# Products with zeros on TensorE in the waits of a decoder step's first projection

## The chip, the cores and the metric

One Trainium2 chip, all 8 of its cores, each with its own share of the tokens and the same program. The metric is device microseconds (us) of the slowest core of an execution. The kernel before takes 744.38 us (median of 3 executions, 744.08 to 744.72).

A program on all cores has a second, slower state in some executions, in which the cores of one die (0 to 3 or 4 to 7) run at a lower granted clock. Only fast executions are compared below, except where a table says that it reads the cores of the undisturbed die.

The engines: PE is TensorE (matmuls and transposes), DVE is VectorE, ACT is ScalarE, POOL is GpSimd, SP issues DMA. "Granted clock" is the profile's figure for PE's clock, as a share of the full one. I call a stretch of PE cold when its 128x512 matmuls start 0.43 us apart (core 2 of before: eleven in 4.90 us at 26.47 us) and warm when they start 0.216 us apart (eight in 1.89 us at 87.02 us).

## The reference

One layer of a hybrid decoder. Only the beginning matters here:

```python
mod = (jax.nn.silu(c) @ w_ada + b_ada)[:, None, :]            # shift, scale, gate, twice
sh1, sc1, gt1, sh2, sc2, gt2 = jnp.split(mod, 6, axis=-1)
h = rmsnorm(x, g_pre_mix) * (1 + sc1) + sh1
proj = h @ w_in                                                # the first projection
v_pool, x_conv, gate_b, gate_c = jnp.split(proj, ...)          # pooling mixer | gated short conv
y_pool = pool_mixer(...); y_conv = gate_b * causal_dwconv(gate_c * x_conv, conv_w)
x = x + gt1 * rmsnorm(concat(y_pool, y_conv) @ w_out, g_post_mix)
# ... then a gated FFN with its own short conv: ~600 us of the ~742, untouched by the change
```

The tokens of a core come in 17 tiles of 128 rows and fewer. A tile is loaded (`big<-x`), its squares are summed on ACT, it is scaled on DVE (`xn`), turned by eight transposes on PE, and copied out of PSUM into `ah`. Matmuls of `ah` with the weights (`ring`) follow. Between them stand small "scale products" of the conditioning vector (`sc`) with weights `wsc_0` to `wsc_7`, each of which is needed before its part of the projection can start.

## The kernel before

The kernel is written as a list of operations with their data; a list scheduler of its own puts them in order with a model of their costs, and each engine's list is then emitted strictly in that order, with semaphore waits.

```python
    def emit(self, eng, e):                     # one engine's instructions, in the scheduler's order
        waited = {}
        for o in self.ops[eng]:
            need = {}
            for d in o.deps: ...                # highest count needed of each semaphore
            for s, v in need.items():
                if waited.get(s, 0) < v:
                    e.wait_ge(s.h, v)
                    waited[s] = v
            r = o.fn(e)
```

```python
    # order(): before 70 us of model time a load also waits for the load that landed last in the model
                if o.dma:
                    under += o.nbytes
                    if last is not None and t <= self.UNTIL:
                        o.deps.add(last)
```

```python
    def load_x(t, src_d, reads=(), deps=()):    # a tile of x into one of six buffers in turn
        i = turn(xts)
        load(BIG[i][0:rows, :], src_d[r0:r0 + rows, :], [r_big[i]], rows * 4096, ...)
        return i

    def stats(src, rows, k, t, reads, junk, junk_regs):      # ACT: sum of squares, then the root
        act(junk, src, AF.Square, reads, [r_stat[k][t]] + junk_regs, D, accum=STAT[0:rows, k, t:t + 1])
        act(STAT[0:rows, k + 1, t:t + 1], STAT[0:rows, k, t:t + 1], AF.Sqrt, ...)

    def turn_tile(t, j, eng):                                # PE: eight transposes into one PSUM bank
        b = take()
        psb = PSF[:, b, :].bitcast(BF16).rearrange("p (k n) -> p k n", k=KC)
        tr([psb[:, kc, 0:rows] for kc in range(KC)], [XN[j][...] for kc in range(KC)], IDB, ..., [r_bank[b]], 0.5)
        ...                                                  # copy to AH on ACT or DVE
        give(b)

    def conv_mid(j, c, bs):                                  # first step of the gated conv: ACT empties a bank
        bx, bc, bb = bs
        act(XC[k], PSF[:, bx, :], AF.Identity, [r_bank[bx], r_cb[j]], [r_xc[k]], n, bias=hx)
        give(bx)                                             # the next product may have this bank
        ...
```

All eight banks of the kernel's PSUM tensor (`PSF`, 128 x 8 x 512) are in use through the `take()` and `give()` of such steps. `give(bx)` is why a transpose on PE can have to wait for a copy on ACT (1.31 us on core 2 and 5.30 us on core 7, below).

Of the kernel before, what the change touches and what calls it, by code (L numbers as in the profile page):

```python
# [10 lines left out]
BF16 = mybir.dt.bfloat16  # L11
# [5 lines left out]
KC = 8  # L17
# [41 lines left out]
class Region:  # L59


    __slots__ = ("w", "r", "bank")
# [14 lines left out]
class Sem:  # L77
    __slots__ = ("h", "count")
# [4 lines left out]


class Op:
    __slots__ = ("eng", "fn", "deps", "sig", "need", "dma", "sem", "n", "cost", "nbytes", "idx", "key", "start", "end", "port")


class Sched:
# [8 lines left out]
    def _mk(self, eng, fn, reads, writes, deps, cost):  # L98
        o = Op()
        o.eng, o.fn, o.cost = eng, fn, cost  # L100
        o.sig, o.need, o.dma, o.sem, o.n, o.nbytes = None, False, False, None, 0, 0
        o.port = eng == "pool"
        o.idx = len(self.all)
        d = set(deps)
        for r in reads:
            if r.w is not None:
                d.add(r.w)
            if r.bank:
                d.update(x for x in r.r if x.eng != eng)
        for w in writes:  # L110
            if w.w is not None:
                d.add(w.w)
            d.update(w.r)
        for r in reads:
            r.r.append(o)
        for w in writes:
            w.w = o
            w.r = []
        d.discard(o)
        o.deps = d  # L120
        self.all.append(o)
        return o
# [12 lines left out]

    RATE = 300e3
    DMA_IN, DMA_OUT = 2.0, 1.5
    LIMIT, SHARE, SMALL, UNTIL = 3.0e6, 0.6e6, 0.4e6, 70.0

    def order(self):  # L140
# [99 lines left out]
                done(o)  # L240
        self.makespan = t

    def finalize(self, esems):
        self.order()
        for o in self.all:
            if o.eng == "pe":
                o.deps = {d for d in o.deps if d.eng != "pe"}
        for o in self.all:
            for d in o.deps:
                d.need = True  # L250
        for e in self.ENGS:
            cnt = 0
            for o in self.ops[e]:
                if o.need and not o.dma:
                    cnt += 1
                    o.sig = (esems[e], cnt)

    def emit(self, eng, e):
        waited = {}
        for o in self.ops[eng]:  # L260
            need = {}
            for d in o.deps:
                s, v = d.sig
                if need.get(s, 0) < v:
                    need[s] = v
            for s, v in need.items():
                if waited.get(s, 0) < v:
                    e.wait_ge(s.h, v)
                    waited[s] = v
            if o.fn is None:  # L270
                continue
            r = o.fn(e)
            if o.dma:
                assert len(r) == o.n, (len(r), o.n)
                for i in r:
                    i.then_inc(o.sem.h, 16)
            elif o.need:
                r.then_inc(o.sig[0].h, 1)


def build_program():
# [42 lines left out]
    def alloc(name, shape, dtype, at=None):  # L324
        esz = 4 if dtype == F32 else 2
        n = esz
        for s in shape[1:]:
            n *= s
        n = (n + 31) // 32 * 32
        off = cur[0] if at is None else at  # L330
        if at is None:
            cur[0] += n
        assert off + n <= SB_HI, ("SBUF overflow", name, off + n - SB_HI)
        high[0] = max(high[0], off + n)
        k = names.get(name, 0)
        names[name] = k + 1
        return slab("%s_%d" % (name, k), list(shape), dtype, offset=off)[:]
# [3 lines left out]
    SC = alloc("sc", [128, KC, 18], BF16)  # L341
# [34 lines left out]
    XN = [alloc("xn", [128, D], BF16) for _ in range(NXN)]  # L376
# [13 lines left out]
    VS = alloc("vs", [128, 4, NS, PB + DS], F32)  # L390
    POOLW = alloc("poolw", [128, 4, 128], BF16)
    CTS = alloc("cts", [128, KC * 18], F32, at=gt_at)
    p1_end = cur[0]

    cur[0] = mark
# [15 lines left out]
    PSF = es.enter_context(nc.psum_tensor("ps", [128, 8, 512], F32))  # L411

    def new_sem(name):
        return Sem(es.enter_context(nc.semaphore(name)))
# [7 lines left out]
    esems = {e: new_sem("e_" + e) for e in Sched.ENGS}  # L422
    K = Sched()
# [12 lines left out]
    def c_mm(n, k=1):  # L436
        return k * max(0.03, n / 2400.0 + 0.0025)

    bank_free = list(range(8))
    r_bank = [R(bank=True) for _ in range(8)]  # L440
# [3 lines left out]
    def take():  # L444
        for b in bank_free:
            if b in singles:
                bank_free.remove(b)
                return b
        raise AssertionError("out of PSUM banks")
# [9 lines left out]
    def give(*bs):  # L459
        for b in bs:  # L460
            assert b not in bank_free
            bank_free.append(b)

    def mm(bank_ap, pairs, reads, writes, n, first=True, last=True):
        def fn(e):
            inst = None
            for i, (l, r) in enumerate(pairs):
                inst = e.matmul(bank_ap, l, r, start=(first and i == 0), stop=(last and i == len(pairs) - 1))  # L468
            return inst
        return K.op("pe", fn, reads=reads, writes=writes, cost=c_mm(n, len(pairs)))  # L470

    def tr(outs, ins, ident, reads, writes, cost):
        def fn(e):
            inst = None
            for o, i in zip(outs, ins):
                inst = e.transpose(o, i, ident)  # L476
            return inst
        return K.op("pe", fn, reads=reads, writes=writes, cost=cost)
# [28 lines left out]
    def load(dst, src, regs, nbytes, eng="sp", sem=None, reads=(), deps=()):  # L507
        return K.dma(eng, lambda e: [e.dma_start(out=dst, in_=src)], sem or next_misc(), 1, reads=reads, writes=regs,
                     deps=deps, nbytes=nbytes)
# [6 lines left out]
        return o  # L516


    r_vecs, r_vd, r_sc, r_rep, r_idf, r_idb, r_eps, r_invc, r_cts = (R() for _ in range(9))
    load(CTS, cT_d, [r_cts], 128 * 576)  # L520
    load(VECS, vecs_d, [r_vecs], 128 * NV * 4)
# [3 lines left out]
    def _invc(e):  # L525
        inst = None
        for g, w in enumerate(WIN):
# [7 lines left out]
    K.op("dve", lambda e: e.tensor_copy(IDB, IDF), reads=[r_idf], writes=[r_idb], cost=0.2)  # L535
    act(SC.rearrange("p k s -> p (k s)"), CTS, AF.Silu, [r_cts], [r_sc], 144)
    K.op("dve", lambda e: e.tensor_copy(REP[:, :, 0:64].rearrange("p k (s r) -> p k s r", r=DS),
                                        SC[:, :, 1:17].unsqueeze(3).to_broadcast([128, KC, NS, DS])),
         reads=[r_sc], writes=[r_rep], cost=0.7)
# [19 lines left out]
    def tile_rows(t):  # L559
        return (t * 128, 128) if t < 16 else (T, TS)  # L560
# [30 lines left out]
    r_ah = [[R() for _ in range(17)] for _ in range(KC)]  # L591
# [11 lines left out]
    def turn_tile(t, j, eng):  # L603

        r0, rows = tile_rows(t)
        b = take()
        psb = PSF[:, b, :].bitcast(BF16).rearrange("p (k n) -> p k n", k=KC)
        tr([psb[:, kc, 0:rows] for kc in range(KC)], [XN[j][0:rows, kc * 128:(kc + 1) * 128] for kc in range(KC)],
           IDB[0:rows, 0:rows], [r_xn[j], r_idb], [r_bank[b]], 0.5)
        regs = [r_ah[kc][t] for kc in range(KC)]  # L610
        if eng == "act":
            act(AH[:, :, r0:r0 + rows], psb[:, :, 0:rows], AF.Copy, [r_bank[b]], regs, KC * rows)
        else:
            K.op("dve", lambda e: e.tensor_copy(AH[:, :, r0:r0 + rows], psb[:, :, 0:rows]), reads=[r_bank[b]],
                 writes=regs, cost=c_dve(KC * rows, 2.0))
        give(b)
# [24 lines left out]
    def ada_scale(w, r_w, kc, GT, r_m, vd0, g0):  # L641
        b = take()
        ps = PSF[:, b, 0:18]
        mm(ps, [(w[:, k, :], SC[:, k, :]) for k in range(KC)], [r_w, r_sc], [r_bank[b]], 18)
        ts(GT[:, kc, :], ps[:, 0:17], VD[:, vd0 + kc:vd0 + kc + 1], VECS[:, g0 + kc:g0 + kc + 1], ALU.add, ALU.mult,
           [r_bank[b], r_vd, r_vecs], [r_m[kc]], 17)
        give(b)
# [24 lines left out]
    r_winp = [R() for _ in range(KC)]  # L672
# [7 lines left out]
    start_b = {}  # L680
# [8 lines left out]
    def start_mm(kc, c):  # L689
        gs = [g for g in range(4) if (g, c) in start_b]  # L690

        def fn(e):
            inst = None
            for g in gs:
                inst = e.matmul(PSF[:, start_b[g, c], :], WINP[:, kc, g * 128:(g + 1) * 128],  # L695
                                AH[:, kc, c * 512:(c + 1) * 512], start=(kc == 0), stop=(kc == KC - 1))
            return inst
        return K.op("pe", fn, reads=[r_winp[kc]] + [r_ah[kc][t] for t in range(4 * c, 4 * c + 4)],
                    writes=[r_bank[start_b[g, c]] for g in gs], cost=c_mm(512, len(gs)))

    def tile_in(t):
        x_front(t)
# [258 lines left out]
    for step in PROJ.split():  # L961
        name, _, args = step.partition(":")
# [314 lines left out]
            state_outs()  # L1277

    K.op("sp", None, deps=out_ops)
    K.finalize(esems)  # L1280
    print("model makespan %.1f us, %d ops" % (K.makespan, len(K.all)))
    with nc.Block() as block:
        @block.tensor
# [112 lines left out]
```

## Time and profile before

| read in | what | value |
|---|---|---|
| page | PE busy, share of the span; share of the chain that ended last | 93%; 84% |
| stretches of 16 us, core 2 | PE busy in 0-16, 16-32, 32-48, 48-64 | 2.0, 8.6, 9.8, 14.7 us |
| the same | DMA share in 16-128 us | 0.95 to 1.04 |
| timelines | last scale product (`wsc_7`), seven cores; core 7 | 48.4 to 49.9; 45.95 us |
| timelines | first product with `w_gate` (the "gate product", end of the region), eight cores | 136.5 to 138.0 us |

The page of the kernel before (core 2, its slowest core): the span, PE's busy time, PE's busy tenths and its granted clock in 40 slices of 18.6 us, and the chain that ended last.

```profile
span 742.2 us, 12030 instructions; the slowest of 8 cores (740.4 to 742.2 us)
PE 691.0 (93%) x3925; PEld 332.7 (45%) x4000; DVE 469.2 (63%) x624; ACT 328.1 (44%) x576; POOL 271.4 (37%) x293
...
PE   1588889999999999999999999999999999999996
...
PEclk9969999999999999999999999999999999999999
...
PE 84%; DVE 5%; issue 5%; DMA 3%; ACT 1%; POOL 1%; DVEq 0%; SPq 0%; ACTq 0%; POOLq 0%
```

PE is idle only at the left end, and the clock is down only in the third slice. All there is to win lies in the first 140 us.

PE's timeline on core 2 of the kernel before, columns: start in us, duration in us, engine, line, operation, output<-inputs, shapes, count, and in brackets the idle time ahead of it and what ended it.

```profile
26.47 4.90 PE L695 MATMUL ps<-ah_81,ring_70 128*128 128x512 bf16 x11 [0.25 <-issue]
...
45.43 4.64 PE L695 MATMUL ps<-ah_81,ring_70 128*128 128x512 bf16 x14
49.90 0.35 PE L468 MATMUL ps<-sc_45,wsc_7_90 128*128 128x18 bf16 x8
...
85.42 0.61 PE L476 MATMUL ps<-idb_52,xn_99 128*128 128x128 bf16 x8 [1.31 <-ACT xc_105 L489]
...
102.52 3.12 PE L468 MATMUL ps<-ah_81,ring_71 128*128 128x512 bf16 x8 [2.19 <-DVE ah_81 L502]
```

Eleven matmuls take 4.90 us at 26 us: cold. So are those at 45 us, in part. The transposes at 85.42 us are those of tile 14; they wait 1.31 us for the copy `xc_105` on ACT, which empties their bank. At 102.5 us the first eight matmuls of a conv product take 3.12 us instead of 1.89 us: cold again.

The same on core 7 of the same execution, where the clock happened to stay at full in the projection:

```profile
42.93 3.18 PE L695 MATMUL ps<-ah_81,ring_70 128*128 128x512 bf16 x14
45.95 0.35 PE L468 MATMUL ps<-sc_45,wsc_7_90 128*128 128x18 bf16 x8
...
85.91 1.01 PE L476 MATMUL ps<-idb_52,xn_99 128*128 128x128 bf16 x8 [5.30 <-ACT xc_105 L489]
```

Its fourteen matmuls take 3.18 us, not 4.64, and its last scale product comes 3.95 us sooner than on core 2. But its transposes of tile 14 start later than on core 2, after a wait of 5.30 us. ACT's timeline on that core says why: its copy stands behind the squares of tile 15, and those wait for a load.

```profile
83.93 1.06 ACT L489 ACTIVATE xn_100<-big_79 128x1024 bf16<-128x1024 f32 x1 [3.47 <-DMA big_79<-x]
84.89 0.19 ACT L489 ACTIVATION_READ_ACCUMULATOR xn_100<-big_79 128x1 f32 x1
84.98 0.20 ACT L489 ACTIVATE xc_104<-ps 128x64 f32<-128x64 f32 x1
85.09 0.68 ACT L489 ACTIVATE xc_105<-ps,bias_53 128x512 f32<-128x512 f32 x1
```

The squares of tile 15 (`xn_100<-big_79`, the output is scratch) start when tile 15 has landed, and `xc_104` and `xc_105` follow at once: the products they copy had been done since 80.61 us at the latest, when PE came to rest (85.91 less the wait of 5.30 us).

### The profile page before, as it was taken

Reading aid. Unit: us, or ns where it says so; the run is one execution under the profiler, and the core shown is the slowest. Engines: PE = TensorE matmul, PEld = TensorE weight load, DVE = VectorE, ACT = ScalarE, POOL = GpSimd, SP = SyncE. Lnnn points to the kernel's source line nnn. Section 1 sums busy time; section 2 is a strip of 40 time slices with the busy share of each in tenths; the row PEclk is TensorE's granted clock in tenths of the full one; section 3 lists DMA queues with packets and bytes.
Section 4 is the critical chain, followed back from the end, with each engine's and each line's share of the span. In section 5 each row is a group of like instructions: output and inputs, shape, how many; then the busy total and the mean of one; then the engine's idle time right before and its main releaser. Section 6 shows DMA issues by size and latency. Waiting matters only on the chain.

```text
span 742.2 us, 12030 instructions; the slowest of 8 cores (740.4 to 742.2 us)
## 1 busy us (share of the span) xinstructions
PE 691.0 (93%) x3925; PEld 332.7 (45%) x4000; DVE 469.2 (63%) x624; ACT 328.1 (44%) x576; POOL 271.4 (37%) x293
## 2 busy tenths in 40 slices
PE   1588889999999999999999999999999999999996
PEld 1244435544455444444444444445444444444442
DVE  2348688745478889997777511128877777767213
ACT  4526754433477784454454311134444444423111
POOL 2313332232488653434444232223433342322320
PEclk9969999999999999999999999999999999999999
DMA  8999999599868554346989974113335433062422
GB/s 207 187 202 216 204 176 188 102 189 200 229 229 268 202 118 82 57 72 101 149 151 151 208 228 166 57 57 57 59 64 88 76 58 57 1 232 86 137 77 72
DMA packets 25713, 101.33 MB, mean 137 GB/s; under 512 B 3310, under 2 KB 5102, under 8 KB 21812
## 3 DMA queue, kind: packets, MB, share of 16 engines
q0 software_dynamic: 10944, 47.85, 39.8%
q1 hardware_dynamic: 14708, 52.71, 21.6%
q8 instruction: 33, 0.54, 0.3%
q14 instruction: 28, 0.23, 0.1%
HBM read 127.49 MB, written 20.90 MB: 200 GB/s over the span
## 4 chain that ended last, share of the span: by engine, by line
PE 84%; DVE 5%; issue 5%; DMA 3%; ACT 1%; POOL 1%; DVEq 0%; SPq 0%; ACTq 0%; POOLq 0%
PE ps L468 81%; PE ps L695 2%; DMA wsc_2_85<-w_sc 2%; PE ps L476 2%; DMA big_77<-x 1%; DVE big_75 L493 1%; DVE big_79 L493 1%; POOL big_77 L497 0%; DVE ta_107 L493 0%; DVE big_80 L493 0%; DVE ah_81 L502 0%; DVE ah_81 L504 0%; ACT ah_81 L489 0%; DVE by_82 L493 0%; DVE xn_99 L502 0%
## 5 line engine op out<-in xcount | busy, mean ns | idle before, releaser
L468 PE MATMUL ps<-wdn_134,g_135 128*128 128x512 bf16 (+1 forms) x733 | 161.4, 379 | 0.9 <-issue 0.2
L468 PE MATMUL ps<-ah_81,ring_71 128*128 128x512 bf16 (+2 forms) x766 | 148.5, 346 | 5.6 <-DVE ah_81 L502 2.2
L468 PE MATMUL ps<-ah_81,ring_72 128*128 128x512 bf16 (+2 forms) x798 | 148.4, 338 | 2.2 <-DVE big_75 L493 1.1
L468 PE MATMUL ps<-ah_81,ring_70 128*128 128x512 bf16 (+2 forms) x739 | 138.0, 339 | 3.2 <-DVE ah_81 L502 0.9
L468 PEld LDWEIGHTS ps<-wdn_134,g_135 128*128 128x128 bf16 (+1 forms) x748 | 73.3, 99 | 87.1 <-issue 0.8
L468 PEld LDWEIGHTS ps<-ah_81,ring_71 128*128 128x128 bf16 x784 | 67.8, 98 | 80.5 <-issue 6.8
L468 PEld LDWEIGHTS ps<-ah_81,ring_72 128*128 128x128 bf16 x816 | 68.8, 98 | 76.8 <-issue 2.4
L468 PEld LDWEIGHTS ps<-ah_81,ring_70 128*128 128x128 bf16 x752 | 63.6, 98 | 72.0 <-issue 3.6
L586 DVE RECIPROCAL stat_55<-stat_55 128x1 f32<-128x1 f32 (+1 forms) x67 | 10.6, 158 | 121.0 <-ACT stat_55 L489 120.7
L497 POOL TENSOR_TENSOR g_135<-big_75,big_76 128x1024 bf16<-128x1024 f32 x15 | 35.4, 2361 | 65.9 <-DVE big_76 L497 34.4
L497 POOL TENSOR_TENSOR g_135<-big_77,big_78 128x1024 bf16<-128x1024 f32 x15 | 35.4, 2357 | 58.0 <-DVE big_78 L497 32.7
L497 POOL TENSOR_TENSOR g_135<-big_79,big_80 128x1024 bf16<-128x1024 f32 x14 | 33.4, 2383 | 55.3 <-DVE big_80 L497 27.5
L489 ACT ACTIVATE big_80<-ps 128x1024 bf16<-128x1024 f32 (+2 forms) x16 | 15.5, 969 | 73.6 <-PE ps L468 72.7
L493 DVE SCALAR_TENSOR_TENSOR big_75<-ps,vecs_43,big_75 128x1023 f32<-128x1023 f32 (+1 forms) x30 | 38.4, 1278 | 11.8 <-ACT halob_58 L489 4.9
L493 DVE SCALAR_TENSOR_TENSOR big_77<-ps,vecs_43,big_77 128x1023 f32<-128x1023 f32 (+1 forms) x30 | 38.4, 1280 | 11.0 <-ACT halob_58 L489 6.2
L493 DVE SCALAR_TENSOR_TENSOR big_78<-ps,vecs_43,big_78 128x1023 f32<-128x1023 f32 (+1 forms) x30 | 38.4, 1279 | 10.4 <-ACT halo_57 L489 5.0
L493 DVE SCALAR_TENSOR_TENSOR big_76<-ps,vecs_43,big_76 128x1023 f32<-128x1023 f32 (+1 forms) x30 | 38.4, 1279 | 9.3 <-ACT halob_58 L489 4.4
L493 DVE SCALAR_TENSOR_TENSOR big_79<-ps,vecs_43,big_79 128x1023 f32<-128x1023 f32 (+1 forms) x28 | 35.8, 1280 | 12.3 <-ACT halob_58 L489 7.6
L493 DVE SCALAR_TENSOR_TENSOR big_80<-ps,vecs_43,big_80 128x1023 f32<-128x1023 f32 (+1 forms) x28 | 35.8, 1279 | 7.9 <-ACT halob_58 L489 3.6
L489 ACT ACTIVATE big_79<-ps 128x1024 bf16<-128x1024 f32 x14 | 14.3, 1023 | 55.8 <-PE ps L468 54.8
L497 POOL TENSOR_TENSOR big_75<-big_79,big_75 128x256 f32<-128x256 f32 (+1 forms) x16 | 20.0, 1250 | 49.6 <-DVE big_79 L493 30.9
L468 PE MATMUL ps<-wo_138,by_82 128*128 128x512 bf16 (+1 forms) x134 | 31.9, 379 | 0.1
(316 smaller groups left out, 895.2 us busy)
## 6 DMA issues: line engine op xcount, KB each, us to landing
ring_70<-w_up POOLq DMA_DIRECT2D x8, 1024.0 KB, 10.2
ring_71<-w_up POOLq DMA_DIRECT2D x7, 1024.0 KB, 10.9
ring_72<-w_up POOLq DMA_DIRECT2D x7, 1024.0 KB, 10.0
wdn_134<-w_down POOLq DMA_DIRECT2D x11, 512.0 KB, 13.9
y<-big_75 SPq DMA_DIRECT2D x7, 512.0 KB, 3.0
y<-big_76 SPq DMA_DIRECT2D x7, 512.0 KB, 2.6
y<-big_77 SPq DMA_DIRECT2D x7, 512.0 KB, 3.7
big_76<-x SPq DMA_DIRECT2D x6, 512.0 KB, 8.7
```

What stands on the lines that cost most here:

```text
L468: inst = e.matmul(bank_ap, l, r, start=(first and i == 0), stop=(last and i == len(pairs) - 1))
L476: inst = e.transpose(o, i, ident)
L489: return K.op("act", lambda e: e.activation(out=out, in_=in_, func=func, **kw), reads=reads, writes=writes, cost=c_act(n, ptr))
L493: return K.op(eng, lambda e: e.scalar_tensor_tensor(out, in0, s, in1, op0, op1), reads=reads, writes=writes, cost=c_dve(n))
L497: return K.op(eng, lambda e: e.tensor_tensor(out, in0, in1, op), reads=reads, writes=writes, cost=c_dve(n) if eng == "dve" else c_pool(n))
L586: K.op("dve", lambda e: e.reciprocal(STAT[0:rows, k + 1, t:t + 1], STAT[0:rows, k + 1, t:t + 1]), reads=[r_stat[k + 1][t]], writes=[r_stat ...
L695: inst = e.matmul(PSF[:, start_b[g, c], :], WINP[:, kc, g * 128:(g + 1) * 128], AH[:, kc, c * 512:(c + 1) * 512], start=(kc == 0), stop=(k ...
```

## The change

Its intent: keep PE's clock up. The trace of before shows the two rates (0.43 and 0.216 us), and on core 7 it shows cold matmuls behind a wait: after the 5.30 us ahead of tile 14's transposes eight matmuls take 3.57 us, and the granted clock is 0.57 in 84 to 92 us. That zero matmuls in the waits keep the clock up was the assumption; the trace of before does not show it. So wherever the scheduler's model sees PE wait, the change puts matmuls of zeros with zeros into the bank that the next product will start anew, after a wait for that bank's readers and for whatever the model expects early:

```diff
-    def finalize(self, esems):
+    PAD, FILL, PADDED = 0.2139, 0.7, 110.0
+
+    def keep_warm(self, zeros):
+        t = 0.0
+        for o in self.ops["pe"]:
+            gap, end = o.start - t, t
+            t = o.start + o.cost
+            if o.pad is None or gap < 0.5 or o.start > self.PADDED:
+                continue
+            late = {d for d in o.deps if d.end > end + 0.25 and d not in o.full}
+            o.early = [d for d in o.deps - late if d.eng != "pe"] + [zeros]
+            gap = o.start - max([end] + [d.end + self.HOP[d.eng] for d in o.full])
+            o.pads = max(0, int(self.FILL * gap / self.PAD)) if end else self.FIRST
+            zeros.need = True
+
+    def finalize(self, esems, zeros):
         self.order()
+        self.keep_warm(zeros)
 ...                                             # emit():
+        for o in self.ops[eng]:
+            if o.pads:
+                wait(o.early)                   # the bank's readers, and what is early in the model
+                for _ in range(o.pads):
+                    o.pad(e)
+            wait(o.deps)
 ...
+    def padded(o, ap, n, first):
+        o.pad = lambda e: e.matmul(ap, ZERO[:, 0:ap.shape[0]], ZERO[:, 0:n], start=first, stop=first)
+        return o
 ...
+    zeros = K.op("dve", lambda e: e.memset(ZERO, 0.0), cost=0.3)
 ...                                             # padded(...) around transposes, scale and first products
```

That makes 73 zero matmuls of 128x512 in 13 places: 24 ahead of the first transpose, 7, 4, 1, 4, 5, 2, 4, 4 up to about 40 us, then 6, 4, 3, and 5 ahead of the conv product at 100 us. Apart from these and one memset on DVE, the order of every engine is that of before.

More of the change, by code (lines that the diff above doesn't have):

```diff
@@ L85 @@
 class Op:
-    __slots__ = ("eng", "fn", "deps", "sig", "need", "dma", "sem", "n", "cost", "nbytes", "idx", "key", "start", "end", "port")
+    __slots__ = ("eng", "fn", "deps", "sig", "need", "dma", "sem", "n", "cost", "nbytes", "idx", "key", "start", "end", "port", "full", "pad", "pads", "early")
 class Sched:
@@ L103, in _mk @@
         o.idx = len(self.all)
+        o.pad, o.pads, o.early = None, 0, ()
+        o.full = {x for w in writes if w.bank for x in w.r + [w.w] if x is not None and x.eng != "pe"}
         d = set(deps)
@@ L137 @@
     DMA_IN, DMA_OUT = 2.0, 1.5
+    FIRST = 24
     LIMIT, SHARE, SMALL, UNTIL = 3.0e6, 0.6e6, 0.4e6, 70.0
@@ L259, in emit, with wait @@
         waited = {}
-        for o in self.ops[eng]:
+        def wait(deps):
             need = {}
-            for d in o.deps:
+            for d in deps:
                 s, v = d.sig
@@ L392, in build_program @@
     CTS = alloc("cts", [128, KC * 18], F32, at=gt_at)
+    ZERO = alloc("zero", [128, 512], BF16)
     p1_end = cur[0]
@@ L469, in fn @@
             return inst
-        return K.op("pe", fn, reads=reads, writes=writes, cost=c_mm(n, len(pairs)))
+        return padded(K.op("pe", fn, reads=reads, writes=writes, cost=c_mm(n, len(pairs))), bank_ap, n, first)
     def tr(outs, ins, ident, reads, writes, cost):
@@ L607, in turn_tile @@
         psb = PSF[:, b, :].bitcast(BF16).rearrange("p (k n) -> p k n", k=KC)
-        tr([psb[:, kc, 0:rows] for kc in range(KC)], [XN[j][0:rows, kc * 128:(kc + 1) * 128] for kc in range(KC)],
+        o = tr([psb[:, kc, 0:rows] for kc in range(KC)], [XN[j][0:rows, kc * 128:(kc + 1) * 128] for kc in range(KC)],
            IDB[0:rows, 0:rows], [r_xn[j], r_idb], [r_bank[b]], 0.5)
+        padded(o, PSF[:, b, :], 512, True)
         regs = [r_ah[kc][t] for kc in range(KC)]
@@ L643, in ada_scale @@
         ps = PSF[:, b, 0:18]
-        mm(ps, [(w[:, k, :], SC[:, k, :]) for k in range(KC)], [r_w, r_sc], [r_bank[b]], 18)
+        o = mm(ps, [(w[:, k, :], SC[:, k, :]) for k in range(KC)], [r_w, r_sc], [r_bank[b]], 18)
+        padded(o, PSF[:, b, :], 512, True)
         ts(GT[:, kc, :], ps[:, 0:17], VD[:, vd0 + kc:vd0 + kc + 1], VECS[:, g0 + kc:g0 + kc + 1], ALU.add, ALU.mult,
@@ L697, in fn @@
             return inst
-        return K.op("pe", fn, reads=[r_winp[kc]] + [r_ah[kc][t] for t in range(4 * c, 4 * c + 4)],
-                    writes=[r_bank[start_b[g, c]] for g in gs], cost=c_mm(512, len(gs)))
+        o = K.op("pe", fn, reads=[r_winp[kc]] + [r_ah[kc][t] for t in range(4 * c, 4 * c + 4)],
+                 writes=[r_bank[start_b[g, c]] for g in gs], cost=c_mm(512, len(gs)))
+        return padded(o, PSF[:, start_b[gs[0], c], :], 512, kc == 0)
     def tile_in(t):
@@ L1279, in build_program @@
     K.op("sp", None, deps=out_ops)
-    K.finalize(esems)
+    K.finalize(esems, zeros)
     print("model makespan %.1f us, %d ops" % (K.makespan, len(K.all)))
```

## The prediction

> **What bounds the kernel now.** PE is 93% busy and 84% of the chain that ended last (the page). Only the first 140 us have idle PE: the stretch table by 16 us shows PE busy 2.0, 8.6, 9.8, 14.7, 14.8, 11.3, 13.8, 15.8, 14.9 of 16, while the DMA share is about 1.0 from 8 to 128 us. In that region the kernel is limited by arrivals (x tiles, projection weights), with the ACT/DVE/POOL conv chain next.
>
> The clock: in the PE timeline of core 2 the first-projection matmuls start 0.43 us apart at 26.5-31 us and again at 37-48 us (granted clock 0.50 there), against 0.216 us elsewhere; a third cold stretch is 102.5-107 us. Together about 8 us of PE time. [...]
>
> **What the change does.** The instruction order of ACT, POOL and SP is unchanged, and that of PE and DVE apart from one memset of zeros and 73 zero matmuls (128x512) in 13 places: 24 before the first transpose, 7, 4, 1, 4, 5, 2, 4, 4 up to about 40 us, then 6, 4, 3, and 5 before the conv matmuls at 102 us. At 0.216 us warm they take about 16 us (the 24 at the start, partly cold, fit inside the 11.4 us wait). Most fall into waits; those before the third scale product, and before the conv product after the projection, stand where the trace has no wait and cost about 1 us each.
>
> **Why I expect little.** Core 7 of the profile before is the experiment already made: there the clock stayed at 1.00 from 31 to 80 us. It finished the projection about 4 us sooner (last scale product at 45.95 us against 49.90), was 3.5 us ahead at 72.7, and then waited 5.3 us at 80.6 for ACT, which waited for an x tile landing at 83.85 us; loads there are chained, landing to issue, without PE. That wait chilled the clock (85-92 us cold), and at the gate product core 7 stood at 137.69 us, core 0 at 137.79, core 2 at 137.98. The change puts no zeros at that wait (the model saw none). So I expect every core to look like core 7: projection 4-6 us sooner, a wait of 4-7 us near 78-85 us, cold there; then warm at 102 us thanks to the five zeros, of which DVE and POOL give back most (core 7's conv chain ran 1.4 us late at 102 us and level at 134). After 140 us nothing changes: all cores need about 604 us from the gate product to the end.
>
> Net gain 0 to 2 us, most likely 0.8. Predicted 743.6 us, range 741.2 to 745.2. Chances: faster 0.01, same 0.98, slower 0.01.
>
> **What would show it.** Clock 1.00 from about 15 to 75 us on all cores; projection matmuls 0.216 us apart from 26 us; last scale product at 43-46 us; a new PE wait of over 3 us before a transpose near 78-85 us, ended by ACT/an x load; cold matmuls after it; gate product at 136-138 us on the slowest core.
>
> **What would make it wrong.** If the x tile lands by 80 us as on core 1 (core 7's late landing being contention), up to 3 us more is kept, and the time could reach 740. If zeros do not count as activity, the clock stays cold, the pads last twice as long, and time rises by 1-3 us.

The forecast's sum came to a net gain of about 0.8 us, 743.6 us against the 744.38 us of before.

## The result and the profile after

| | median | executions | ratio to before, 95% interval |
|---|---|---|---|
| before | 744.23 us | 743.96 to 744.72, 4 | |
| after | 744.06 us | 742.99 to 745.02, 4 | 0.9997 (0.9979 to 1.0014) |
| after, again in the last batch below, on another chip | 744.07 us | 743.50 to 745.71, 6 | 0.9981 (0.9957 to 1.0006) |

A ratio here is the mean time of one kernel's fast executions over that of the other's of the same rounds, so it is not quite the ratio of the medians. The result is correct, and the time is the same.

The page after (core 6, the slowest), the same lines as before:

```profile
span 742.7 us, 12179 instructions; the slowest of 8 cores (738.4 to 742.7 us)
PE 706.0 (95%) x3997; PEld 338.2 (46%) x4073; DVE 470.0 (63%) x625; ACT 328.3 (44%) x576; POOL 271.1 (36%) x293
...
PE   6689699999999999999999999999999999999996
...
PEclk9799899999999999999999999999999999999999
...
PE 79%; DMA 10%; issue 4%; DVE 3%; POOL 1%; ACT 1%; DVEq 0%; SPq 0%; ACTq 0%; POOLq 0%
PE ps L501 78%; DMA big_79<-x 2%; DMA wsc_2_85<-w_sc 2%; DMA big_77<-x 2%; DMA big_78<-x 1%; DMA big_76<-x 1%; DMA wsh_2_93<-w_sh 1%; PE ps L509 1%; DMA ring_70<-w_inp 1%; DVE big_79 L526 1%; DVE big_75 L526 0%; POOL big_77 L530 0%; POOL ta_106 L530 0%; DVE ss_112 L530 0%; DVE npp_118 L535 0%
```

PE is busier by 15 us of zeros. The clock's dip has moved from the third slice to the second and fifth. DMA has gone from 3% to 10% of the chain that ended last, and `big_79<-x`, the load of tile 15, is at the head of it. The time that PE gained was handed to a wait for a load.

PE's timeline on core 6 of after; the lines answer to those of core 2 before:

```profile
1.90 7.93 PE L494 MATMUL ps<-zero_134 128*128 128x512 bf16 x24 [1.90 <-DVE zero_134 L552]
...
22.75 1.91 PE L494 MATMUL ps<-zero_134 128*128 128x512 bf16 x4
26.49 0.36 PE L501 MATMUL ps<-sc_45,wsc_2_85 128*128 128x18 bf16 x8 [1.83 <-DMA wsc_2_85<-w_sc]
...
28.38 3.22 PE L731 MATMUL ps<-ah_81,ring_70 128*128 128x512 bf16 x8 [0.22 <-issue]
...
43.22 3.18 PE L731 MATMUL ps<-ah_81,ring_70 128*128 128x512 bf16 x14
46.24 0.35 PE L501 MATMUL ps<-sc_45,wsc_7_90 128*128 128x18 bf16 x8
...
86.18 1.01 PE L509 MATMUL ps<-idb_52,xn_99 128*128 128x128 bf16 x8 [5.08 <-ACT xc_105 L522]
...
88.14 3.57 PE L501 MATMUL ps<-ah_81,ring_71 128*128 128x512 bf16 x8
```

The fourteen matmuls ahead of the last scale product take 3.18 us, as on core 7 of before, and that product comes at 46.24 us. Then the transposes of tile 14 wait 5.08 us for `xc_105`, and what follows is cold: 3.57 us for eight matmuls. ACT on the same core:

```profile
79.59 0.29 ACT L522 ACTIVATE stat_55<-stat_55,eps_69 128x1 f32<-128x1 f32 x1
84.20 1.06 ACT L522 ACTIVATE xn_100<-big_79 128x1024 bf16<-128x1024 f32 x1 [4.32 <-DMA big_79<-x]
85.16 0.19 ACT L522 ACTIVATION_READ_ACCUMULATOR xn_100<-big_79 128x1 f32 x1
85.26 0.20 ACT L522 ACTIVATE xc_104<-ps 128x64 f32<-128x64 f32 x1
85.36 0.68 ACT L522 ACTIVATE xc_105<-ps,bias_53 128x512 f32<-128x512 f32 x1
```

It is the picture of core 7 of before, now on all eight cores: ACT waits 3.1 to 4.9 us for tile 15 on each of them. The chain in order of time on core 6 (start, duration, what) has it as one link of two loads of x:

```profile
60.12 9.48 DMA big_76<-x
69.68 14.38 DMA big_79<-x
```

How much of the gain survives depends on when that load lands:

| core of after | last scale product | squares of tile 15 start | tile 14's transposes [wait] | gate product | span |
|---|---|---|---|---|---|
| 4 | 43.52 | 80.56 | 82.54 [2.83] | 133.57 | 738.4 |
| 0 | 45.27 | 81.60 | 83.58 [3.51] | 134.68 | 739.4 |
| 3 | 42.83 | 82.78 | 84.76 [4.94] | 136.20 | 740.5 |
| 6 | 46.24 | 84.20 | 86.18 [5.08] | 138.22 | 742.7 |
| before, core 2 | 49.90 | 81.13 | 85.42 [1.31] | 137.98 | 742.2 |

These four stand for all eight: the order of the spans is that of the landings (core 5 alone is out of order, by 0.7 us), not that of the scale products, where core 3 was the first. After the gate product every core of both kernels needs 603.9 to 604.8 us to the end. So in this pair of profiles a median core gained: the median of the eight spans fell from 741.55 to 739.3 us. The slowest did not, and the metric is the slowest. This is one execution of each kernel. In the control of the third batch, over all fast executions, the median core gains 1.2 us and the slowest 1.4 us.

The cores also differ at the start. The first big product was cold on all eight cores before (4.8 to 5.3 us for 11 or 12 matmuls). After, it was warm on cores 1 to 5 (2.75 to 2.86 us for 12) and cold, at least in part, on cores 0, 6 and 7. Core 2 of after:

```profile
26.01 2.75 PE L731 MATMUL ps<-ah_81,ring_70 128*128 128x512 bf16 x12
```

The last scale product comes at 42.8 to 43.9 us on the five and at 45.3 to 46.2 us on the three.

### The profile page after: what moved, and what is told of

Read it like the earlier page. It is cut to its first block, busy times and chain, and to the rows that moved or that the text cites. A ratio compares the mean times of both kernels' runs of the same rounds, so it can differ in the third digit from the quotient of the medians.

```text
span 742.7 us, 12179 instructions; the slowest of 8 cores (738.4 to 742.7 us)
## 1 busy us (share of the span) xinstructions
PE 706.0 (95%) x3997; PEld 338.2 (46%) x4073; DVE 470.0 (63%) x625; ACT 328.3 (44%) x576; POOL 271.1 (36%) x293
## 4 chain that ended last, share of the span: by engine, by line
PE 79%; DMA 10%; issue 4%; DVE 3%; POOL 1%; ACT 1%; DVEq 0%; SPq 0%; ACTq 0%; POOLq 0%
PE ps L501 78%; DMA big_79<-x 2%; DMA wsc_2_85<-w_sc 2%; DMA big_77<-x 2%; DMA big_78<-x 1%; DMA big_76<-x 1%; DMA wsh_2_93<-w_sh 1%; PE ps L509 1%; DMA ring_70<-w_inp 1%; DVE big_79 L526 1%; DVE big_75 L526 0%; POOL big_77 L530 0%; POOL ta_106 L530 0%; DVE ss_112 L530 0%; DVE npp_118 L535 0%
## 5 line engine op out<-in xcount | busy, mean ns | idle before, releaser
L530 POOL TENSOR_TENSOR g_136<-big_75,big_76 128x1024 bf16<-128x1024 f32 x15 | 35.4, 2357 | 65.4 <-DVE big_76 L530 34.1
L526 DVE SCALAR_TENSOR_TENSOR big_79<-ps,vecs_43,big_79 128x1023 f32<-128x1023 f32 (+1 forms) x28 | 35.8, 1280 | 12.5 <-ACT halob_58 L522 7.8
```

Source lines behind the costliest of these rows:

```text
L526: return K.op(eng, lambda e: e.scalar_tensor_tensor(out, in0, s, in1, op0, op1), reads=reads, writes=writes, cost=c_dve(n))
L530: return K.op(eng, lambda e: e.tensor_tensor(out, in0, in1, op), reads=reads, writes=writes, cost=c_dve(n) if eng == "dve" else c_pool(n))
```

## The experiments

Theory W (the load wait): the zeros make the projection warm and about 4 us shorter, PE then arrives at tile 14 before tile 15 has landed, and ACT, which starts `xc_105` only behind the squares of tile 15 (85.36 behind 84.20 us on core 6 of after), holds up the bank that PE needs. What the zeros gave is handed to a load. Rival C: the zeros cost as much PE time as they save. Rival S: the load is late because other loads share the DMA engines with it. Rival N: the warm clock of the projection is worth nothing to the end at all.

The idea of filling the new wait with zeros as well was not measured. The bank the transposes will use is the one being waited for, and a version with zeros into unused columns of a bank that another engine reads was refused by a check for races before it could run; no run on record shows that attempt.

### First batch

All four kernels fell on a chip whose die 1 was slow in nearly every execution (before: 755.38 us median). Their total times are not used. I read cores 0 to 3 of the profiled executions, which were undisturbed.

**swap_before, swap_after.** ACT's squares of tile 15 are moved four places down, to just ahead of their own root; nothing else moves. In both kernels:

```diff
         self.order()
+        sq, rt = self.late                     # squares and root of tile 15
+        acts = self.ops["act"]
+        acts.remove(sq)
+        acts.insert(acts.index(rt), sq)
```

> The kernel before, with one ScalarE instruction (the squares of tile 15) moved four places later, behind the first two conv copies. Theory (the zeros' lead is thrown away at a wait for tile 15 of x, which sits ahead of those copies in ScalarE's queue): without the zeros PE is too late for that wait to matter on 7 of 8 cores, so nothing moves: 743.5 to 744.6 us, ratio 0.999 to 1.001. Rival (that order in ScalarE's queue costs by itself, zeros or not): 2 to 3 us faster, as in swap_after.

> The changed kernel with the same move. Theory: PE's wait before the transposes of tile 14 falls from 2.8-5.1 us to under 2 us, those transposes start at 79-82.5 us instead of 82.5-86, no cold matmuls follow, and the time falls to 740.5-742 us (ratio to before 0.995 to 0.997). Rival 1 (the zeros' own 16 us of PE work eat the gain): the wait shrinks but the time stays near 744. Rival 2 (the conv chain on VectorE and GpSimd gives any lead back): the transposes come 3 us sooner, the gate product at 137-138 us as before, time 744.

Measured: in the kernel with zeros the wait ahead of tile 14's transposes was 1.36 us on all four cores, and they started at 80.1 to 81.9 us instead of 82.5 to 86.2. The gate product came at 133.5 to 134.7 us, the spans were 738.1 to 739.5 us. Without zeros the four spans were 738.2, 744.4, 742.0 and 740.4 us; three of these cores were warm in the projection by chance (last scale product 45.9 to 46.2 us), so this run says little about a cold core. The first half of theory W holds: the ACT queue passes the load's lateness to PE. The totals (754.36 and 756.19 us) belong to the slow die and decide nothing.

**hold_after.** The kernel with zeros, with the eight loads of `w_ss` held until tile 15 has landed:

```diff
-        load(W2[kc]..., wss_d[kc], [r_w2[kc]], 1 << 20, eng="pool")
+        K.held[1].append(load(W2[kc]..., wss_d[kc], [r_w2[kc]], 1 << 20, eng="pool"))
...
+        for o in self.held[1]:
+            o.deps.add(self.held[0])           # the load of tile 15
```

> The changed kernel with the eight loads of the second modulation's weights (w_ss, 512 KB each) held back until tile 15 of x has landed; no order changes. If tile 15 lands late because those loads share the DMA engines with it: it lands 7 to 10 us after issue instead of 10-15, by 78 us on all cores, ScalarE's wait for it is under 1 us, and the time is 741-742 us. If it lands late only because the loads are chained one behind the other: landing stays at 80-84 us and the time at 744.

Measured: the squares of tile 15 started at 78.2 to 82.4 us on cores 0 to 3 after waits of 2.75 to 3.18 us, and the spans were 737.9 to 742.1 us. The wait is still there, although the trace shows these loads issued at 78.7 us and later (cores 0 and 3) instead of from 67.8 us: sharing with them is not what makes tile 15 late, or at most a microsecond of it (the squares start at 80.75 us in the mean of the four cores, at 81.84 in the changed kernel). Rival S falls for `w_ss`; the other loads of that time were not tried.

**zeros_double.** `FILL` 1.4 instead of 0.7, which makes 58 zeros more, in the same places:

```diff
-    PAD, FILL, PADDED = 0.2139, 0.7, 110.0
+    PAD, FILL, PADDED = 0.2139, 1.4, 110.0
```

> The changed kernel with the share of each modelled wait that is filled doubled from 0.7 to 1.4: 58 zero matmuls more, about 12.5 us of PE work, in 12 places. Theory (PE's time before 78 us is slack, since it waits for tile 15 anyway): the last scale product comes 3 to 6 us later than in the changed kernel, the wait near 80 us shrinks by as much, the time stays within 0.1% of the changed kernel's, 743.5-745 us. Rival 1 (the zeros' own work sits in the way): the time rises by 3 us or more, to 747.

Measured: spans of 742.9, 745.1, 745.1, 745.0 us on cores 0 to 3. PE's timeline on core 2 of this run (the trace names tiles without numbers); the second line is the transposes that came at 74.1 to 76.9 us in the changed kernel, the last ones before tile 14's:

```profile
72.11 1.68 PE L494 MATMUL ps<-zero 128*128 128x512 bf16 x7
...
82.55 0.61 PE L509 MATMUL ps<-idb,xn 128*128 128x128 bf16 x8 [0.25 <-ACT v L522]
...
88.07 0.61 PE L509 MATMUL ps<-idb,xn 128*128 128x128 bf16 x8 [1.36 <-ACT xc L522]
```

The wait for tile 15 is gone, because PE now arrives later than the load, and the gate product is at 138.2 to 140.4 us. The last scale product came 4.6 us later on average (47.2 to 49.2 us), as expected, but the time was not unchanged: the four spans average 744.5 us against 739.6 in the changed kernel, about 5 us more, on another chip. So part of the added zeros (12.5 us, an estimate from 58 times 0.216) was slack and part was not. That is what rival C would look like, and at 0.7 the kernel does not look like it: there PE arrives early and waits 3 to 5 us.

### Second batch: the load wait and the five late zeros

On another chip (before: 745.69 us median, 743.79 to 746.73, 11 executions). From here on, medians are those of the fast executions.

**swap2_before, swap2_after.** Both instructions of tile 15 on ACT, squares and root, are moved behind the first three conv copies:

```diff
         self.order()
+        acts = self.ops["act"]
+        for o in self.late:                    # squares and root of tile 15
+            acts.remove(o)
+        i = acts.index(self.copy) + 1          # the third of the first conv copies
+        acts[i:i] = self.late
```

> The kernel before, with both ScalarE instructions of tile 15's statistics moved behind the first three conv copies. In the first four runs one die was slow throughout, so only its other die told something: there the one-instruction move took PE's wait before tile 14's transposes to 1.4 us with the zeros and left another of 2 us just after. Theory: without the zeros most cores come too late for tile 15 to matter, so this is within 0.15% of before: 743.2-744.8 us. Rival (the order costs by itself): 741-742 us.

> The changed kernel with the same move. Theory: no core waits for tile 15 any more at that place; both waits of PE there are under 1.5 us, the gate product comes at 132-134.5 us on every core, spans 736-739.5, and the slowest core stops being an outlier: 740-741.5 us, ratio to before 0.994 to 0.996. If the lead is given back later in the conv chain: gate product at 137 us, time 744.

Measured: without zeros 744.33 us, ratio 0.9982 (0.9969 to 0.9995); with zeros 741.75 us, ratio 0.9954 (0.9939 to 0.9968), one execution in the slow state left out. With zeros the wait ahead of tile 14's transposes was 1.3 to 2.8 us and the gate product came at 132.2 to 136.4 us. That is more waiting and a wider spread than I expected with zeros (under 1.5 us, 132 to 134.5 us); the ratio was as expected, the time 0.25 us above the range. The same edit gives more where the zeros are in. Once it is made, the zeros are worth 2.1 us on this chip (means of the fast executions, 744.13 and 742.01).

**unchain_after.** The loads of tiles 12 to 15 no longer wait for an earlier load to land, only for their buffers:

```diff
-        p1a[t] = norm_tile(t, load_x(t, x_d, deps=deps), ST1)
+        xi = load_x(t, x_d, deps=deps)
+        if t >= 12:
+            o = r_big[xi].w
+            K.free.append((o, set(o.deps)))
+        p1a[t] = norm_tile(t, xi, ST1)
...
         self.order()
+        for o, own in self.free:
+            o.deps &= own
```

> The changed kernel with the loads of tiles 12 to 15 of x freed of their wait for the landing of an earlier load (they still wait for their buffers); no order changes. If the chain of landings is what makes tile 15 late: it is issued at 64-66 us instead of 67-70 and lands at 77-79 instead of 80-84, ScalarE's wait for it is under 2 us, spans 737-739.5, time 741-742. If the DMA engines' bandwidth is the limit, the earlier issue lands no earlier, because tile 14 and the others slow down: 743.5-744.5.

Measured: 740.68 us, ratio 0.9936 (0.9919 to 0.9952), one execution in the slow state left out. But the profiled execution, the slowest of its fast ones with 742.98 us, does not show the mechanism I had in mind. Three loads of x, tile 15 the last of them, were now issued within 1.8 to 3.5 us instead of 5.9 to 6.8 us, and still ACT's squares of tile 15 started at 78.8 to 83.5 us, mean 81.0, after waits of 1.8 to 5.3 us; in after_again (below) the mean is 82.0 us. The DMA share was 1.03 in 64 to 96 us before and after the change already; tile 15 issued about 5 us sooner lands about 1 us sooner. The time fell by more than this one profile explains; how is open. This is the one result that theory W does not account for: the wait is still there, and the kernel is as fast as with it gone.

**no_five.** The changed kernel without the five zeros at 99 us:

```diff
-    PAD, FILL, PADDED = 0.2139, 0.7, 110.0
+    PAD, FILL, PADDED = 0.2139, 0.7, 80.0
```

> The changed kernel without the last group of zeros (five, before the conv products at 100-102 us). My prediction said that VectorE and GpSimd give most of these back: then those conv products are cold again (about 3.1 us for eight instead of 1.9) but the gate product and the time differ by less than 0.5 us from the changed kernel. If the five are what the change lives on: 2 us slower than the changed kernel on every core, spans 741-744.

Measured: 744.73 us, ratio 0.9989 (0.9975 to 1.0002). In the changed kernel, core 0, the five zeros and the conv product behind them:

```profile
99.14 1.24 PE L494 MATMUL ps<-zero_134 128*128 128x512 bf16 x5 [0.71 <-ACT by_82 L522]
100.63 1.89 PE L501 MATMUL ps<-ah_81,ring_71 128*128 128x512 bf16 x8 [0.25 <-DVE ah_81 L535]
```

Without them, core 0 of no_five:

```profile
103.11 3.08 PE L501 MATMUL ps<-ah,ring 128*128 128x512 bf16 x8 [2.30 <-DVE ah L535]
```

The eight matmuls of the product take 3.08 us instead of 1.89: cold. From the start of this product to the gate product it is 34.04 us where it starts warm (core 0 of after: 134.68 - 100.63 = 34.05; core 7 of before: 33.99; cores 3 and 5 of no_five, which were warm: 34.04) and 35.4 to 35.6 us where it starts cold (the other cores of no_five; core 2 of before, 137.98 - 102.52 = 35.46). So on a core that would be cold there the five zeros are worth about 1.4 us at the gate product. In the total times that is not visible on its own: the intervals of no_five and of the changed kernel (0.9957 to 1.0006, on another chip) overlap. The spans of the profile, 741.5 to 743.1 us, are those of the second branch of the expectation. The median core gains 0.6 us over the kernel before without the five and 1.2 us with them (each against the kernel before on its own chip), so a good part of what the change leaves may be theirs; that is not settled.

### Third batch: the two cures with and without zeros

I call the edits of swap2 and unchain the two cures. All four kernels ran on one further chip (before: 745.36 us median, 743.68 to 749.59, 10 fast executions), 5 rounds each.

**unchain_swap2**: the changed kernel with the edits of swap2 and unchain together. **unchain_swap2_before**: the kernel before with the same two edits, so without a single zero. **unchain_before**: the kernel before with freed loads alone. **after_again**: the changed kernel as it stands. The diffs are those above.

> The changed kernel with both cures of the load wait: the loads of x tiles 12 to 15 wait for their buffers alone, and ScalarE's two statistics instructions of tile 15 stand behind the first three conv copies. If both cures take away the same wait, they do not add: 740.5 to 742 us, ratio to before 0.993 to 0.995, TensorE's wait ahead of the transposes of tile 14 under 2.8 us on every core. If they are two waits, they add: 738 to 740 us, ratio under 0.992.

> The same two cures, without a single zero matmul. If the zeros are hidden behind the load wait, then the cured kernel without them must be slower than the cured kernel with them by what a median core gained from them, about 2 us or more: 742.5 to 744 us, ratio 0.996 to 0.9985. If the zeros are worth nothing to the time and the cures make the whole gain, it equals the cured kernel with zeros within 0.6 us.

> The kernel before with freed loads alone, no zeros. If the load wait binds only a core whose projection is warm, freeing the loads gains under 1 us here (743.5 to 745 us, ratio 0.998 to 1.000), where it gained about 2.5 us or more in the kernel with zeros. If the load wait binds every core whatever its clock, the gain is the same 2.5 us or more here (ratio under 0.997).

> The changed kernel as it stands, once more, with more rounds and on the same chip as the three others: a control. If its result stands, 743.5 to 745 us, ratio 0.998 to 1.0005, with at least one core of the eight whose tile 15 lands after 83 us and whose span is within 1 us of the kernel before. If the first result was an accident of few runs, it is at 742 us or less.

Measured; the first column of times is the median of the fast executions, and the last two are means over them of the median and of the slowest of the eight spans:

| kernel | zeros | median us | ratio to before (95%) | median core | slowest core |
|---|---|---|---|---|---|
| before | no | 745.36 | | 741.7 | 744.1 |
| after_again | yes | 744.07 | 0.9981 (0.9957 to 1.0006) | 740.5 | 742.8 |
| unchain_before | no | 744.06 | 0.9975 (0.9951 to 0.9998) | 739.6 | 742.4 |
| unchain_swap2_before | no | 744.19 | 0.9978 (0.9952 to 1.0004) | 739.6 | 742.6 |
| unchain_swap2 | yes | 740.68 | 0.9933 (0.9909 to 0.9957) | 737.9 | 739.3 |

By the means of the fast executions (before 745.67 us), zeros alone give 1.4 us, the two cures alone 1.5 us, both together 4.8 us. With the cures in, the zeros are worth 3.4 us (means of 744.20 and 740.84; in ratios 0.9933 / 0.9978 = 0.9955). The zeros' worth with the cures is 2.0 us above that without; the standard error of this difference, from the spread of these executions, is about 0.8 us, so it is clear of noise, but its size is not settled. Rival N falls with that, and so does rival C: the same zeros are neither worthless nor self-consuming once nothing stands in the way.

The profile of unchain_swap2_before settles rival N by itself. From the last scale product to the gate product a core that was warm in the projection takes as long as one that was cold: 87.86 us on core 0 (44.93 to 132.79) and 87.88 us on core 5 (50.37 to 138.25). Nothing of the lead is lost there. And the conv product is warm in both cured kernels, with zeros or without (eight matmuls in 1.89 us on all cores of both), so the five late zeros have no part in the 3.4 us.

Why the cures do little without zeros: they shorten a wait that a cold core does not have. In unchain_before both kinds of core are in one execution. ACT on core 5, which was cold in the projection (last scale product 49.33 us), and then on core 4, which was warm by chance (45.76 us), at the squares of tile 15:

```profile
81.68 1.06 ACT L492 ACTIVATE xn<-big 128x1024 bf16<-128x1024 f32 x1 [1.01 <-DMA big<-x]
```

```profile
81.58 1.06 ACT L492 ACTIVATE xn<-big 128x1024 bf16<-128x1024 f32 x1 [4.50 <-DMA big<-x]
```

The load landed at the same time; only the warm core was there 3.5 us earlier to wait for it. PE waited 1.31 us ahead of tile 14's transposes on core 5 and 3.59 us on core 4.

Why the zeros do much with the cures: they make the last cold cores warm. Two cores of unchain_swap2_before, granted clock third from the right, in the stretches 32 to 40 and 40 to 48 us. First core 5 (span 742.6 us), then core 3 (736.0 us):

```profile
32.00:40.00 8.00, 3.78 (x40) 2.36 (x38) 4.32 (x12) 2.54 (x5) 1.01 (x1) 0.72 1.08 152
40.00:48.00 8.00, 6.51 (x36) 3.06 (x37) 3.60 (x12) 1.02 (x1) 0.00 (x0) 0.50 0.96 224
```

```profile
32.00:40.00 8.00, 3.70 (x44) 2.16 (x40) 3.26 (x10) 3.56 (x6) 0.00 (x0) 1.00 1.07 163
40.00:48.00 8.00, 7.89 (x56) 3.80 (x53) 4.30 (x16) 1.50 (x4) 0.00 (x0) 1.00 0.80 232
```

They ran the same program with the same little work in 32 to 40 us (3.78 and 3.70 us busy); one lost its clock (0.72, then 0.50) and the other did not (1.00). No run here shows what decides between the two. In this profile four cores kept the clock (spans 736.0 to 738.1 us) and four lost it (742.0 to 742.7 us), and in all four fast executions the slowest of the eight had a mean granted clock of 0.99, that of the cores that lost it, where those that kept it had 0.999. Core 5 of unchain_swap2, with the zeros:

```profile
32.00:40.00 8.00, 6.52 (x58) 3.36 (x56) 4.91 (x12) 2.54 (x5) 0.69 (x2) 1.00 1.10 151
40.00:48.00 8.00, 6.62 (x58) 3.55 (x57) 3.83 (x15) 1.02 (x1) 0.00 (x0) 1.00 0.98 229
```

And ACT on core 1 of unchain_swap2, where the wait for tile 15 was:

```profile
80.33 0.68 ACT L530 ACTIVATE xc<-ps,bias 128x512 f32<-128x512 f32 x1
...
81.99 1.04 ACT L530 ACTIVATE xn<-big 128x1024 bf16<-128x1024 f32 x1
```

The conv copy goes first, the squares of tile 15 follow with no wait at all, and PE's transposes wait 1.31 us, there and on the other seven cores. Of the expectations, the first for the two cures together held: they do not add (ratio 0.9933, against 0.9936 for freed loads alone on the other chip), and the waits are all under 2.8 us. The cured kernel without zeros fell where it was expected by its ratio (0.9978) and 0.2 us above it by its time. For freed loads alone without zeros I had expected under 1 us; the ratio of 0.9975 is 1.9 us, with an interval from 0.1 to 3.7 us, so that size is not settled. The control came out as expected (0.9981, and cores 5 and 6 with tile 15 after 83 us).

## Why the prediction was right, and where its steps were not

The time was right (743.6 us predicted, 744.06 measured, range 741.2 to 745.2), and so was the mechanism that carried it: a core with a warm projection is handed on to a wait for tile 15.

- *"last scale product at 43-46 us"*: 42.83 to 46.24 us. Right.
- *"a new PE wait of over 3 us before a transpose near 78-85 us, ended by ACT/an x load"* and *"cold matmuls after it"*: 2.83 to 5.08 us on the eight cores, and eight matmuls in 2.5 to 3.6 us after it. Right; the experiments show it to be the cause, because with the wait taken away the zeros are worth 3.4 us (2.1 us in swap2, where part of the wait is left).
- *"I expect every core to look like core 7"* and *"gate product at 136-138 us on the slowest core"*: the slowest was at 138.22 us, the others at 133.6 to 136.2. Core 7 was an example of a late landing and not of the typical one. The prediction took one core for all and missed that the median core gains (2.2 us in this pair of profiles, 1.2 us in the control); in both profiled executions of the changed kernel some core of the eight had its load land late, and that core set the time. In after_again it was cores 5 and 6, squares of tile 15 at 84.47 and 83.68 us, spans 742.1 and 741.8.
- *"Clock 1.00 from about 15 to 75 us on all cores; projection matmuls 0.216 us apart from 26 us"*: wrong for the clock, and half right for the matmuls. In 16 to 24 us the granted clock was below full on all eight cores (0.58 to 0.89), in spite of the zeros before it, and it came back on core 6 at 31 us only; the eight matmuls at 28.38 us took 3.22 us. Five cores were warm by the first big product at 26 us (2.75 to 2.86 us, above), three were not. From 32 us on the clock was full on all eight. Which groups of zeros did that was not tested one by one.
- *"those before the third scale product, and before the conv product after the projection, stand where the trace has no wait and cost about 1 us each"*: wrong for the first, where the 1.91 us of zeros at 22.75 us were followed by another 1.83 us of waiting for the load of `wsc_2`. The trace before had shown this wait: 2.68 us ahead of the same product at 25.86 us on core 2. Right for the second: four zeros stand between transposes and conv product at 54.3 us, where PE does not wait (0.86 us of four warm starts, an estimate from 0.216 us each).
- *"the five zeros, of which DVE and POOL give most back"*: wrong in size. A cold conv product costs 1.4 us at the gate product (35.46 on core 2 of before against 34.05 us on core 0 of after), so on a cold core that much of it is kept.
- *"Net gain 0 to 2 us, most likely 0.8"*: 0.2 us in the first comparison and 1.4 us in the control; neither interval excludes zero. The hit is luck in part: the prediction had the early clock too good on three cores and the five zeros worth too little, and how far these errors cancel is not shown.

What stays open: why the load of tile 15 lands up to 4 us later on some cores, why freeing the loads alone gave the kernel with zeros as much as it did, and which groups of zeros are needed.

The best versions found are unchain_swap2, 740.68 us and 0.67% below before, and unchain_after, which is level with it (0.9936 on the other chip). They are faster than both kernels, by less than the 2% at which a difference is called one here.

## What to carry to other kernels

A faster stretch is worth what the next wait leaves of it (here 1.4 us with the wait for tile 15 in place, 3.4 us with it cured): before counting a gain, look in the traces for a core that already had it by chance, and see where it lost it. Where engines whose lists are in a fixed order feed each other, an instruction that waits for a load should not stand ahead of one that frees a bank for the busiest engine: on the eight cores of after that order cost PE waits of 2.83 to 5.08 us, and with both cures the wait was 1.31 us. When the metric is the slowest of several cores, a median gain is no gain until the worst core has it, so read all cores, and test two small cures together as well as one by one.

## What the traces show of PE's clock and of ACT's queue

- PE's clock was halved with short idle times. On core 2 of before the longest idle time of PE from 30 us until the granted clock fell from 1.00 to 0.50 at about 34.7 us was 1.69 us (2.35 us if the transposes are not counted as work), and on core 6 of after it fell from 1.00 to 0.50 at about 20.8 us, 1.5 us into an idle time of 2.37 us, with PE busy 1.33 us of the 4 us before 20. How busy PE has to be to keep the clock, no run here shows.
- Matmuls with operands of zero went from cold to warm with nothing else on PE. On core 6 of after 24 zero matmuls alone ran on PE up to 9.8 us, and they took 7.93 us, where the half rate throughout would be 10.3 us (24 times 0.43, an estimate): the first ten took 4.42 us, which is the half rate, and the last eleven 2.54 us, which is the full one. With the zeros in, the granted clock was 1.00 from 32 to 48 us on all eight cores; before, it was 0.57 to 0.59 on seven cores and 1.00 on core 7.
- Early in a trace the distance of the matmuls has to be read, not the granted clock alone: the records of core 2 before give 1.00 from 24 to 32 us, where 11 matmuls took 4.90 us, which is the half rate. Whether a record is missing, or the view shows full clock until the first one, no run here shows.
- ACT's instructions started in the order of its list in the timelines printed here. The price: one instruction waited 3.1 to 4.9 us at the head of that list on all eight cores of after, with `xc_105` behind it.
